# A two-layer attention trunk: accumulator tiles by token tile, grouped value products, earlier pairs, an ordered end

## The chip, the cores and the metric

The kernel runs on one core of one Trainium2 chip. The metric is the device time of one execution in microseconds (us); the median of several executions is compared. The profile shown is of one execution.

## What is computed

Two decoder layers over 256 tokens with 1024 features, in float32. Each layer normalises its input, multiplies it with one wide input projection, and cuts the result into heads of 64 columns:

```python
def even_layer(x, mem, norm_g, w_in, qk_g, sinks, mem_norm_g, w_mem_kv, w_out):
    h = rms_norm(x, norm_g)
    aq, ak, av, bq, bk, bv, mq, z = split_cols(h @ w_in, EVEN_SPLIT)
    ...
    y = jnp.concatenate([ya, yb, ym], axis=-1) * jax.nn.silu(z)
    return x + y @ w_out

def odd_layer(x, mem, norm_g, w_in, qk_g, b_f, mem_norm_g, w_mem_kv, w_out):
    h = rms_norm(x, norm_g)
    cq, ck, cv, cf, mq, z = split_cols(h @ w_in, ODD_SPLIT)
    ...
    y = jnp.concatenate([yc, ym], axis=-1) * jax.nn.silu(z)
    return x + y @ w_out
```

Layer 0 has 6 heads of sliding-window attention (`ya`, two key and value heads), 6 heads of causal attention over one block of 256 (`yb`) and 4 heads that look at a memory of 256 rows (`ym`). Layer 1 has 12 heads of forgetting attention (`yc`) and again 4 memory heads. Queries and keys are normalised per head; the head outputs are multiplied by the SiLU of the gate `z`, and an output projection adds into the residual.

## The kernel before

**Projections.** All projections are cut into chunks of up to 512 columns (`ch0` to `ch3`, `z0`, `z1`, `mem0`, `mem1`, `out00`, `out01` for layer 0; `cfmq`, `y1`, `va`, `qka`, `qb`, `kb`, `vb`, `y0`, `out10`, `out11` for layer 1). The 1024 rows of the contraction are eight blocks of 128 (k = 0 to 7), and a chunk is four pieces of two blocks. `emit_dma` loads a piece, `emit_prep` splits it into a rounded part and a rest (a ScalarE cast, L276, and a VectorE subtraction, L277), and `emit_mm` multiplies it. Tokens are two tiles of 128 (t = 0, 1). For each block and token tile there are three TensorE products of 512 columns: rounded by rounded (L315), rounded by rest (L316), rest by rounded (L317). A chunk accumulates in one PSUM tile `acc` of 128x2x512, two banks, from a pool with two buffers. In a chunk's first and last piece the products of t = 0 stand ahead of those of t = 1. After the last piece the chunk's `post` function reads `acc`.

**Pairs of heads.** Attention goes by pairs of heads, 16 of them: `a0` to `a2`, `b0` to `b2`, `m00`, `m01` in layer 0, `m10`, `m11`, `c0` to `c5` in layer 1. A pair has three units of work: `scores` (TensorE products, VectorE minimum, ScalarE exponential), `transp` (TensorE transposes of the probabilities of head f = 0 and f = 1, each copied by ScalarE into a tile `pT`, L531), and `values`. There, each head's products have 64 output rows, so that f = 0 goes to the lower and f = 1 to the upper half of the columns of the array; each of the four products (two key tiles kt, two heads) is two records in the trace. Then GpSimd scales the gate (L550), TensorE transposes it (L554), ScalarE copies the values out (L556), VectorE multiplies (L557), and the result is split into `yT` hi and lo (L193, L194), which the output projection reads, one block k for each pair.

**Order.** Units stand in a queue `units`; after each piece one or two are taken off (`pump`), and ahead of a piece of an output projection as many as it needs. A pair's `transp` and `values` are put into the queue when the next pair is added (`add_pair`) or when `end_pairs` is called, which happens after `mem0` and after `kb`. In layer 1 that means that `m11` waits in `pend` until `c4` is added (after `qka`), and `c5` until `c0` is added (after `kb`). The last projection takes its pieces alternately from `out10` and `out11`, in the order of blocks (6, 7), (4, 5), (0, 1), (2, 3); blocks 0 to 3 are pairs `c0` to `c3`.

A planner then fixes the order of every engine's instructions: it simulates the engines, and gives an engine the instruction that is ready and stands first in the source. Once fixed, the order on an engine does not change on the chip. [...]

Of the kernel before, what the change touches and what calls it, by code (L numbers as in the profile page):

```python
# [2 lines left out]

# [6 lines left out]
F32 = mybir.dt.float32  # L10
F32R = mybir.dt.float32r
AF = mybir.ActivationFunctionType
# [4 lines left out]
P = 128  # L17
# [32 lines left out]
def tile_hybrid_trunk(  # L50
# [13 lines left out]
    qkp = ctx.enter_context(tc.tile_pool(name="qkp", bufs=2))  # L64
    wk = ctx.enter_context(tc.tile_pool(name="wk", bufs=2))
    st = ctx.enter_context(tc.tile_pool(name="st", bufs=3))
    ps_acc = ctx.enter_context(tc.tile_pool(name="ps_acc", bufs=2, space=PSUM))
    ps_at = ctx.enter_context(tc.tile_pool(name="ps_at", bufs=4, space=PSUM))

    nc.scalar.preload_act_table_set("natural_log_exp_and_others")  # L70


    ident = const.tile([P, P], F32, name="ident")
# [220 lines left out]
    def emit_mm(i):  # L294
        c, p = pieces[i]
        hi, lo = preps.pop(i)
        aT = c.act()
        if p == 0:
            c.acc = ps_acc.tile([P, 2, 512], F32, tag="acc", name=f"acc_{c.name}")
        ks = range(c.kts[p][0], c.kts[p][1] + 1)  # L300
        steps = [(j, k, t) for j, k in enumerate(ks) for t in range(2)]
        if p in (0, NPIECE - 1):
            steps.sort(key=lambda x: x[2])
        for j, k, t in steps:
            a_hi = aT[0][:, k, t * P:(t + 1) * P]
            a_lo = aT[1][:, k, t * P:(t + 1) * P]
            o = c.acc[:, t, :c.n]
            first = p == 0 and j == 0
            last = p == NPIECE - 1 and j == PIECE_KT - 1

            parts = 2 if last and t == 1 and i == len(pieces) - 1 else 1
            w = c.n // parts
            for q in range(parts):
                qq = slice(q * w, (q + 1) * w)
                nc.tensor.matmul(o[:, qq], a_hi, hi[:, j, qq], start=first, stop=False)  # L315
                nc.tensor.matmul(o[:, qq], a_hi, lo[:, j, qq], start=False, stop=False)  # L316
                nc.tensor.matmul(o[:, qq], a_lo, hi[:, j, qq], start=False,  # L317
                                 stop=last and q == parts - 1)
        if p == NPIECE - 1:
            with tc.high_priority(offset=POST):  # L320
                c.post(c.acc)


    def qk_post(acc, c0, n, cs, rms, name, blocks, perm_a=False, mid=None):
        w = n * HD
        sq = wk.tile([P, 2, 512], F32, tag="sq", bufs=SQ_BUFS, name=f"qsq_{name}")
        nc.scalar.activation(sq[:, :, :w], acc[:, :, c0:c0 + w], AF.Square)
        if mid:
            mid()
        ss = st.tile([P, 2, n], F32, tag="ss", name=f"qss_{name}")  # L330
        nc.vector.tensor_reduce(ss, sq[:, :, :w].rearrange("p t (h d) -> p t h d", d=HD),
                                axis=AX.X, op=ALU.add)
        v = st.tile([P, 2 * n], F32, tag="vv", name=f"qv_{name}")
        for t in range(2):
            nc.vector.scalar_tensor_tensor(v[:, t * n:(t + 1) * n], ss[:, t, :],
                                           rms.ev[:, t:t + 1], cs[:, :n],
                                           op0=ALU.add, op1=ALU.mult)
        r = rsqrt_(v, 2 * n, name)
        qn = wk.tile([P, 2, 512], F32, tag="sq", bufs=SQ_BUFS, name=f"qn_{name}")
        r3 = r.rearrange("p (t h) -> p t h", t=2)  # L340
        for t in range(2):
            rb = r3[:, t, :, None].broadcast_to([P, n, HD])
            src = acc[:, t, c0:c0 + w].rearrange("p (h d) -> p h d", d=HD)
            if perm_a:
                dst = qn[:, t, 0:384].rearrange("p (i f d) -> p f i d", f=2, d=HD)
                for f in range(2):
                    nc.vector.tensor_mul(dst[:, f], src[:, 3 * f:3 * f + 3, :],
                                         rb[:, 3 * f:3 * f + 3, :])
                nc.vector.tensor_mul(qn[:, t, 384:512].rearrange("p (h d) -> p h d", d=HD),
                                     src[:, 6:8, :], rb[:, 6:8, :])  # L350
            else:
                nc.vector.tensor_mul(qn[:, t, :w].rearrange("p (h d) -> p h d", d=HD), src, rb)  # L352
        b0 = 0
        for kind, key, nb, gain in blocks:
            for g in range(0, nb, 2):
                m = min(2, nb - g)
                tp = ps_at.tile([P, 2, 256], F32, tag="at", name=f"qt_{name}_{b0}_{g}")
                for j in range(m):
                    for t in range(2):
                        b = b0 + g + j  # L360
                        nc.tensor.transpose(tp[:, j, t * P:(t + 1) * P],
                                            qn[:, t, b * P:(b + 1) * P], ident)
                (q_parts if kind == "q" else k_parts)(key, g, tp, m, gain)
            b0 += nb
# [57 lines left out]

    def v_post(acc, c0, n, rms, dst):
        for t in range(2):
            nc.vector.tensor_scalar_mul(dst[:, t, :], acc[:, t, c0:c0 + n], rms.r[:, t:t + 1])

    def silu_post(acc, rms, zs):
        for t in range(2):
            nc.vector.tensor_scalar_mul(zs[:, t, :], acc[:, t, :], rms.r[:, t:t + 1])
        s = wk.tile([P, 2, 512], F32, tag="sq", bufs=SQ_BUFS, name="sg")  # L430
        nc.scalar.activation(s, zs, AF.Exp, scale=-1.0)
        nc.scalar.activation(s, s, AF.Ln, bias=ones_c)
        nc.scalar.activation(s, s, AF.Exp, scale=-1.0)
        nc.vector.tensor_mul(zs, zs, s)  # L434
# [5 lines left out]
    def pump(n=1):  # L440
        while n > 0 and units:
            ready, fn = units[0]
            if not ready():
                return
            units.pop(0)
            fn()
            n -= 1
# [15 lines left out]
    class Pair:  # L463
# [70 lines left out]
        def values(self):  # L534
# [2 lines left out]
            nc.vector.reciprocal(rec, self.sums)  # L537
            o = ps_at.tile([P, 2, 256], F32, tag="at", name=f"o_{self.name}")
            v = self.v()
            for kt in range(2):  # L540
                q0 = 0 if (full or kt == 0) else P
                for f in range(2):
                    c = self.vcols[f]
                    nc.tensor.matmul(o[f * HD:(f + 1) * HD, 0, q0:256], v[:, kt, c:c + HD],  # L544
                                     self.pT[f][:, 256 * kt:256 * kt + 256 - q0],
                                     start=kt == 0, stop=kt == 1)
            zs = wk.tile([P, 2, P], F32, tag="zs", name=f"zs_{self.name}")
            zsil = zsils[self.layer]
            for t in range(2):
# [78 lines left out]
    def post_out(layer, half):  # L628
        def f(acc):
            dst = xt[:, :, 512 * half:512 * half + 512]  # L630
            if layer == 1:
                for t in range(2):
                    parts = 2 if half == 1 and t == 1 else 1
                    w = 512 // parts
                    for q in range(parts):
                        qq = slice(q * w, (q + 1) * w)
                        tag, b = ("pT", PT_BUFS) if half and t else ("p", 4)
                        o = wk.tile([P, 512], F32, tag=tag, name=f"o_{half}_{t}_{q}", bufs=b)
                        nc.vector.tensor_add(o[:, :w], acc[:, t, qq], dst[:, t, qq])
                        nc.sync.dma_start(out[t * P:(t + 1) * P,  # L640
                                              512 * half + q * w:512 * half + (q + 1) * w],
                                          o[:, :w])
                return
# [3 lines left out]
            with tc.high_priority(offset=HOIST):  # L647
                for j in range(2):
                    cc = slice(256 * j, 256 * j + 256)
                    nc.vector.tensor_add(dst[:, :, cc], acc[:, :, cc], dst[:, :, cc])  # L650
                    hi = turn_x1(hTs[1], 4 * half + 2 * j)
                with tc.issue_after(hi.ins):
                    for t in range(2):
# [11 lines left out]
    def post_cfmq(acc):  # L665
        xf = st.tile([P, 2, 12], F32, tag="f1", name="xf", bufs=1)
        for t in range(2):
            nc.vector.scalar_tensor_tensor(xf[:, t, :], acc[:, t, 0:12], R[1].r[:, t:t + 1], bfc,
                                           op0=ALU.mult, op1=ALU.add)
        qk_post(acc, 12, 4, cs_one, R[1], "cfmq", [("q", "mq1", 2, gq[:, 8:9])])  # L670
        add_mem_pairs(1, lambda: "y1" in done)
        a = st.tile([P, 2, 12], F32, tag="f2", name="fa", bufs=1)
        nc.vector.scalar_tensor_tensor(a, xf, -1.0, xf, op0=ALU.mult, op1=ALU.max)
        e = st.tile([P, 2, 12], F32, tag="f3", name="fe", bufs=1)
# [36 lines left out]
    def post_qka(acc):  # L711
        qk_post(acc, 0, 8, cs_one, R[1], "qka",
                [("q", "qa", 2, gq[:, 6:7]), ("k", "ka", 2, gcol[:, 7:8])])
        for j in (4, 5):
            add_fox(j, "qa", "ka", lambda: T["va"], j - 4)

    def post_va(acc):
        T["va"] = qkp.tile([P, 2, 256], F32, tag="mv", name="va", bufs=3)
# [94 lines left out]
    for i in range(len(pieces)):  # L813
# [21 lines left out]
        if c.name.startswith("out"):  # L835
            need = [f"o{c.name[3]}_{k}" for k in c.kts[p]]
            while not all(n in done for n in need):
                before = len(units)
                pump(1)
                assert len(units) < before  # L840
        emit_mm(i)
        pump(2 if len(units) > BACKLOG else 1)


# [28 lines left out]
```

## Time and profile before

| | |
|---|---|
| median of 3 runs | 294.77 us (294.49 to 295.39) |
| the profiled execution | 294.83 us |
| its span, first to last instruction | 293.1 us |
| TensorE busy | 283.6 us, 97% |
| VectorE busy | 217.4 us, 74% |
| ScalarE busy | 210.1 us, 72% |
| GpSimd busy | 49.1 us, 17% |
| mean granted TensorE clock | 0.998 of full speed |

The span is 1.7 us shorter than the execution's own time. Engine names are PE (TensorE products), PEld (its weight loads), DVE (VectorE), ACT (ScalarE), POOL (GpSimd), SP (the queue that issues the weight loads and the stores). A busy PE counts overlapping products once; the time from one product's start to the next one's start tells what a product really takes from the engine.

### The profile page before, as it was taken

How to read it: one execution, taken by the hardware profiler on the slowest of the kernel's cores; microseconds unless marked ns; L12 is line 12 of the kernel's file. 1: busy time of each engine (PE TensorE's matmuls, PEld its weight loads, DVE VectorE, ACT ScalarE, POOL GpSimd, SP SyncE). 2: the span in 40 equal slices, each digit the busy share in tenths (PEclk: the TensorE clock that was granted, in tenths of full speed). 3: DMA queues.
4: the chain of work that ended last, by engine and by line, in shares of the span. 5: the costliest groups of instructions: out<-in, count | busy, mean ns of one | idle time of the engine just before them, and what ended most of it. 6: DMA issues, size and time to landing. Idle time of an engine off the chain costs nothing.

```text
span 293.1 us, 4507 instructions
## 1 busy us (share of the span) xinstructions
PE 283.6 (97%) x1479; PEld 225.9 (77%) x1479; DVE 217.4 (74%) x474; ACT 210.1 (72%) x435; POOL 49.1 (17%) x113
## 2 busy tenths in 40 slices
PE   7799999999999999999999999999999999999993
PEld 4568887888787777877678989878887788777773
DVE  2567999879997986795638889958698789645423
ACT  3667895999779959767627649956678799668520
POOL 9920000000501000291000000460100220012100
PEclk9999999999999999999999999999999999999999
DMA  6967746442625362443126456586635524630003
GB/s 205 307 226 267 219 144 215 145 143 93 205 72 193 91 202 83 144 145 110 41 73 196 130 158 200 130 261 166 197 104 184 147 70 144 215 114 33 0 2 143
DMA packets 24871, 43.37 MB, mean 148 GB/s; under 512 B 1904, under 2 KB 6288, under 8 KB 24848
## 3 DMA queue, kind: packets, MB, share of 16 engines
q1 hardware_dynamic: 24544, 43.05, 47.0%
q0 software_dynamic: 288, 0.03, 0.5%
q8 instruction: 12, 0.20, 0.2%
q14 instruction: 11, 0.09, 0.1%
q10 hardware_dynamic: 16, 0.00, 0.0%
HBM read 42.02 MB, written 1.05 MB: 147 GB/s over the span
## 4 chain that ended last, share of the span: by engine, by line
PE 82%; DMA 7%; DVE 5%; ACT 2%; issue 2%; SPq 0%; DVEq 0%; ACTq 0%
DMA raw_ch<-in_e_w_in_dram 6%; PE acc_out L315 5%; PE acc_out L317 5%; PE acc_out L316 5%; PE acc_mem L315 3%; PE acc_ch L315 3%; PE acc_ch L317 3%; PE acc_y L316 3%; PE acc_ch L316 3%; PE acc_y L315 2%; PE acc_mem L317 2%; PE acc_mem L316 2%; PE acc_y L317 2%; PE o_c L544 2%; DVE wlo_ch L277 2%; PE o_m L544 2%
## 5 line engine op out<-in xcount | busy, mean ns | idle before, releaser
L277 DVE TENSOR_TENSOR wlo_ch<-raw_ch,whi_ch 128x1024 fp32r<-128x1024 f32 (+1 forms) x17 | 19.7, 1165 | 12.5 <-ACT whi_ch L276 12.4
L315 PE MATMUL acc_out<-whi_out,yT_hi 128*128 128x512 f32 (+1 forms) x65 | 26.3, 404 | 0.0
L316 PE MATMUL acc_ch<-wlo_ch,hT_hi 128*128 128x512 f32 x64 | 25.4, 397 | 0.6 <-DVE wlo_ch L277 0.6
L277 DVE TENSOR_TENSOR wlo_out<-raw_out,whi_out 128x1024 fp32r<-128x1024 f32 x16 | 20.4, 1280 | 7.2 <-ACT whi_out L276 7.1
L316 PE MATMUL acc_out<-wlo_out,yT_hi 128*128 128x512 f32 (+1 forms) x65 | 25.7, 396 | 0.0
L315 PE MATMUL acc_ch<-whi_ch,hT_hi 128*128 128x512 f32 x64 | 25.3, 396 | 0.2 <-DVE qn_ch L352 0.2
L317 PE MATMUL acc_ch<-whi_ch,hT_lo 128*128 128x512 f32 x64 | 25.4, 397 | 0.0
L317 PE MATMUL acc_out<-whi_out,yT_lo 128*128 128x512 f32 (+1 forms) x65 | 25.0, 397 | 0.0
L276 ACT CAST whi_ch<-raw_ch 128x1024 fp32r<-128x1024 f32 (+1 forms) x17 | 16.9, 994 | 9.9 <-DMA raw_ch<-in_e_w_in_dram 9.9
L276 ACT CAST whi_out<-raw_out 128x1024 fp32r<-128x1024 f32 x16 | 16.7, 1046 | 2.1 <-DMA raw_out<-in_o_w_out_dram 1.1
L509 ACT ACTIVATE p_c<-p_c,nm_c 128x128 f32<-128x128 f32 (+1 forms) x24 | 10.8, 451 | 5.8 <-DVE nm_c L502 5.8
L316 PEld LDWEIGHTS acc_ch<-wlo_ch,hT_hi 128*128 128x128 f32 x64 | 12.0, 188 | 3.6 <-DVE wlo_ch L277 1.3
L315 PEld LDWEIGHTS acc_out<-whi_out,yT_hi 128*128 128x128 f32 x65 | 12.2, 188 | 2.9 <-ACT yT_hi L193 0.4
L550 POOL TENSOR_TENSOR zs_c<-z,rec_c 128x128 f32<-128x128 f32 x12 | 5.5, 485 | 53.6 <-DVE z L434 26.3
L315 PEld LDWEIGHTS acc_ch<-whi_ch,hT_hi 128*128 128x128 f32 x64 | 12.0, 188 | 3.0 <-issue 0.6
L317 PEld LDWEIGHTS acc_out<-whi_out,yT_lo 128*128 128x128 f32 x65 | 12.2, 188 | 2.8 <-issue 0.4
L317 PEld LDWEIGHTS acc_ch<-whi_ch,hT_lo 128*128 128x128 f32 x64 | 12.0, 188 | 2.9 <-issue 0.4
L316 PEld LDWEIGHTS acc_out<-wlo_out,yT_hi 128*128 128x128 f32 x65 | 12.3, 189 | 2.5 <-issue 0.4
L550 POOL TENSOR_TENSOR zs_a<-z,rec_a 128x128 f32<-128x128 f32 x6 | 4.2, 727 | 56.7 <-PE acc_ch L317 56.4
L315 PE MATMUL acc_mem<-whi_mem,hmT_hi 128*128 128x512 f32 x32 | 12.9, 403 | 0.0
L315 PE MATMUL acc_z<-whi_z,hT_hi 128*128 128x512 f32 x32 | 12.9, 402 | 0.0
L316 PE MATMUL acc_z<-wlo_z,hT_hi 128*128 128x512 f32 x32 | 12.7, 398 | 0.0
(380 smaller groups left out, 880.7 us busy)
## 6 DMA issues: line engine op xcount, KB each, us to landing
raw_ch<-in_e_w_in_dram SPq DMA_DIRECT2D x15, 512.0 KB, 4.5
raw_z<-in_e_w_in_dram SPq DMA_DIRECT2D x8, 512.0 KB, 4.0
raw_y<-in_o_w_in_dram SPq DMA_DIRECT2D x8, 512.0 KB, 3.7
raw_out<-in_o_w_out_dram SPq DMA_DIRECT2D x8, 512.0 KB, 3.9
raw_mem<-in_e_w_mem_kv_dram SPq DMA_DIRECT2D x4, 512.0 KB, 3.4
raw_mem<-in_o_w_mem_kv_dram SPq DMA_DIRECT2D x4, 512.0 KB, 3.4
raw_out<-in_e_w_out_dram SPq DMA_DIRECT2D x4, 512.0 KB, 3.7
raw_qka<-in_o_w_in_dram SPq DMA_DIRECT2D x8, 256.0 KB, 3.0
```

The lines of the kernel that those rows point to most:

```text
L276: op = nc.scalar.copy(hi[:, jj, :c.n], raw[:, jj, :c.n])
L277: nc.vector.tensor_sub(lo[:, jj, :c.n], raw[:, jj, :c.n], hi[:, jj, :c.n].bitcast(F32))
L315: nc.tensor.matmul(o[:, qq], a_hi, hi[:, j, qq], start=first, stop=False)
L316: nc.tensor.matmul(o[:, qq], a_hi, lo[:, j, qq], start=False, stop=False)
L317: nc.tensor.matmul(o[:, qq], a_lo, hi[:, j, qq], start=False, stop=last and q == parts - 1)
L509: nc.scalar.activation(pt[:, a:b], src[:, a:b], AF.Exp, scale=-1.0, bias=nm[:, f, t:t + 1], accum_out=sums[:, f, t:t + 1])
L544: nc.tensor.matmul(o[f * HD:(f + 1) * HD, 0, q0:256], v[:, kt, c:c + HD], self.pT[f][:, 256 * kt:256 * kt + 256 - q0], start=kt == 0, stop ...
L550: nc.gpsimd.tensor_mul(zs[:, t, :].rearrange("p (f d) -> p f d", d=HD), self.zsel(zsil, t), rec[:, :, t:t + 1].broadcast_to([P, 2, HD]))
```

## The change

Four things. The accumulator `acc` becomes two tiles of 128x512, one for each token tile, from a pool of four one-bank buffers; whatever reads `acc` for both token tiles in one instruction becomes two instructions (the squares of `qk_post`, the residual addition of layer 0). In `values` the first product is that of kt = 0, f = 1, and the other three are told to the planner as standing behind it on TensorE. `end_pairs` is also called after the memory pairs of layer 1 and after `qka`. The last two pieces (blocks 2 and 3 of `out10` and `out11`) and their stores are emitted together under `in_order`, which ties each instruction to the one before it on its engine, in source order.

```diff
-    ps_acc = ctx.enter_context(tc.tile_pool(name="ps_acc", bufs=2, space=PSUM))
+    ps_acc = ctx.enter_context(tc.tile_pool(name="ps_acc", bufs=4, space=PSUM))
...
+    @contextmanager
+    def in_order():
+
+        traced = nc.cur_bb.bb.instructions
+        n = len(traced)
+        yield
+        last = {}
+        for i in traced[n:]:
+            if i.engine in last:
+                tc.add_manual_dep(
+                    i, last[i.engine],
+                    mybir.DependencyInfo(mybir.DependencyClass.NoSync,
+                                         mybir.DependencyReason.DATA),
+                    reason="in_order")
+            last[i.engine] = i.name
...
-            c.acc = ps_acc.tile([P, 2, 512], F32, tag="acc", name=f"acc_{c.name}")
+            c.acc = [ps_acc.tile([P, 512], F32, tag="acc", name=f"acc_{c.name}_{t}")
+                     for t in range(2)]
...
-            o = c.acc[:, t, :c.n]
+            o = c.acc[t][:, :c.n]
...
-        nc.scalar.activation(sq[:, :, :w], acc[:, :, c0:c0 + w], AF.Square)
+        for t in range(2):
+            nc.scalar.activation(sq[:, t, :w], acc[t][:, c0:c0 + w], AF.Square)
...
-            for kt in range(2):
+
+            def value(kt, f):
                 q0 = 0 if (full or kt == 0) else P
-                for f in range(2):
-                    c = self.vcols[f]
-                    nc.tensor.matmul(o[f * HD:(f + 1) * HD, 0, q0:256], v[:, kt, c:c + HD],
-                                     self.pT[f][:, 256 * kt:256 * kt + 256 - q0],
-                                     start=kt == 0, stop=kt == 1)
+                c = self.vcols[f]
+                return nc.tensor.matmul(o[f * HD:(f + 1) * HD, 0, q0:256], v[:, kt, c:c + HD],
+                                        self.pT[f][:, 256 * kt:256 * kt + 256 - q0],
+                                        start=kt == 0, stop=kt == 1)
+
+            lead = value(0, 1)
+            with tc.issue_after(lead.ins):
+                value(0, 0)
+                value(1, 1)
+                value(1, 0)
...
-                    nc.vector.tensor_add(dst[:, :, cc], acc[:, :, cc], dst[:, :, cc])
+                    for t in range(2):
+                        nc.vector.tensor_add(dst[:, t, cc], acc[t][:, cc], dst[:, t, cc])
...
         add_mem_pairs(1, lambda: "y1" in done)
+        end_pairs()
...
             add_fox(j, "qa", "ka", lambda: T["va"], j - 4)
+        end_pairs()
...
-        emit_mm(i)
-        pump(2 if len(units) > BACKLOG else 1)
+        if i < len(pieces) - 2:
+            emit_mm(i)
+            pump(2 if len(units) > BACKLOG else 1)
+
+    n = len(pieces)
+    with in_order():
+        emit_mm(n - 2)
+        emit_mm(n - 1)
```

The remaining lines of the diff only follow the new shape of `acc` (`acc[:, t, ...]` becomes `acc[t][:, ...]`).

## Rows read from the trace of the kernel before

**Rows 1.** The page's first part: busy time, share of span, instructions.

```profile
PE 283.6 (97%) x1479; PEld 225.9 (77%) x1479; DVE 217.4 (74%) x474; ACT 210.1 (72%) x435; POOL 49.1 (17%) x113
```

**Rows 2.** Busy time by stretch: stretch, length, engines with instructions, clock, DMA share, GB/s.

```profile
60.00:100.00 40.00, 40.00 (x210) 31.71 (x208) 35.78 (x89) 35.89 (x80) 5.47 (x10) 1.00 0.43 138
...
190.00:224.00 34.00, 34.00 (x178) 27.53 (x177) 25.92 (x44) 22.50 (x38) 7.39 (x10) 1.00 0.65 200
...
282.00:293.10 11.10, 6.60 (x36) 4.96 (x31) 3.49 (x7) 0.78 (x2) 0.00 (x0) 0.96 0.26 96
```

**Rows 3.** The waits of PE: total us, times, longest us.

```profile
PE tp_x L222 <- DMA xt<-in_x_dram: 2.1, 2, 1.4
```

**Rows 4.** Timeline of PE around one pair's values: start, length, instruction.

```profile
101.16 0.40 PE L315 MATMUL acc_z<-whi_z,hT_hi 128*128 128x512 f32 x1
101.49 0.65 PE L544 MATMUL o_b<-pT_b,bv 128*64 128x256 f32 x2
102.06 0.51 PE L316 MATMUL acc_z<-wlo_z,hT_hi 128*128 128x512 f32 x1
102.41 0.40 PE L317 MATMUL acc_z<-whi_z,hT_lo 128*128 128x512 f32 x1
102.64 0.40 PE L315 MATMUL acc_z<-whi_z,hT_hi 128*128 128x512 f32 x1
...
105.50 0.86 PE L544 MATMUL o_b<-pT_b,bv 128*64 128x256 f32 x6
```

**Rows 5.** Chain of waits, value products: end of the piece before, share of path, records.

```profile
66.28 0.80 PE o_a L544 x8
...
74.62 0.58 PE o_a L544 x2
...
76.54 0.79 PE o_a L544 x5
...
274.41 0.57 PE o_c L544 x2
```

**Rows 6.** Groups by line and shape, ACT and DVE: count, busy us, mean ns.

```profile
L327 ACT ACTIVATE qsq_qka<-acc_qka 128x1024 f32<-128x1024 f32 x1 | 1.0, 1027 | 1.7 <-PE acc_qka L317 1.7
...
L327 ACT ACTIVATE qsq_cfmq<-acc_cfmq 128x512 f32<-128x512 f32 x1 | 0.6, 592 | 0.0
...
L650 DVE TENSOR_TENSOR xt<-acc_out,xt 128x512 f32<-128x512 f32 x4 | 2.6, 686 | 1.7 <-PE acc_out L317 1.7
...
L639 DVE TENSOR_TENSOR o<-acc_out,xt 128x256 f32<-128x256 f32 x2 | 0.7, 414 | 0.0
```

**Rows 7.** Timeline near 47 us, PE at the start of chunk ch2.

```profile
46.51 1.02 DVE L352 TENSOR_TENSOR qn_ch<-acc_ch,r_ch 128x384 f32<-128x384 f32 x2
...
47.08 0.40 PE L317 MATMUL acc_z<-whi_z,hT_lo 128*128 128x512 f32 x1
...
47.68 0.47 PE L315 MATMUL acc_ch<-whi_ch,hT_hi 128*128 128x512 f32 x1 [0.21 <-DVE qn_ch L352]
```

**Rows 8.** Timeline of the last pair, from its values to its first use.

```profile
281.56 0.87 PE L544 MATMUL o_c<-pT_c,vb 128*64 128x256 f32 x8
...
282.56 0.48 PE L315 MATMUL acc_out<-whi_out,yT_hi 128*128 128x512 f32 x1
...
283.57 0.63 PE L317 MATMUL acc_out<-whi_out,yT_lo 128*128 128x512 f32 x2
283.76 0.41 ACT L193 CAST yT_hi<-ob_c 128x256 fp32r<-128x256 f32 x1 [0.49 <-DVE ob_c L557]
284.19 0.43 DVE L194 TENSOR_TENSOR yT_lo<-ob_c,yT_hi 128x256 fp32r<-128x256 f32 x1 [0.47 <-ACT yT_hi L193]
...
284.21 0.50 PE L315 MATMUL acc_out<-whi_out,yT_hi 128*128 128x512 f32 x1
```

**Rows 9.** Timeline of the end: last product, last additions, stores.

```profile
287.76 2.92 SPq L640 DMA_DIRECT2D out_dram<-o  x5
...
288.34 0.28 PE L317 MATMUL acc_out<-whi_out,yT_lo 128*128 128x256 f32 x1
288.65 1.35 DVE L639 TENSOR_TENSOR o<-acc_out,xt 128x512 f32<-128x512 f32 x3 [0.33 <-PE acc_out L317]
```

More of the change, by code (lines that the diff above doesn't have):

```diff
@@ L1 @@
 import math
-from contextlib import ExitStack
+from contextlib import ExitStack, contextmanager
 import concourse.bass as bass
@@ L342, in qk_post @@
             rb = r3[:, t, :, None].broadcast_to([P, n, HD])
-            src = acc[:, t, c0:c0 + w].rearrange("p (h d) -> p h d", d=HD)
+            src = acc[t][:, c0:c0 + w].rearrange("p (h d) -> p h d", d=HD)
             if perm_a:
@@ L424, in v_post @@
         for t in range(2):
-            nc.vector.tensor_scalar_mul(dst[:, t, :], acc[:, t, c0:c0 + n], rms.r[:, t:t + 1])
+            nc.vector.tensor_scalar_mul(dst[:, t, :], acc[t][:, c0:c0 + n], rms.r[:, t:t + 1])
     def silu_post(acc, rms, zs):
         for t in range(2):
-            nc.vector.tensor_scalar_mul(zs[:, t, :], acc[:, t, :], rms.r[:, t:t + 1])
+            nc.vector.tensor_scalar_mul(zs[:, t, :], acc[t], rms.r[:, t:t + 1])
         s = wk.tile([P, 2, 512], F32, tag="sq", bufs=SQ_BUFS, name="sg")
@@ L638, in f @@
                         o = wk.tile([P, 512], F32, tag=tag, name=f"o_{half}_{t}_{q}", bufs=b)
-                        nc.vector.tensor_add(o[:, :w], acc[:, t, qq], dst[:, t, qq])
+                        nc.vector.tensor_add(o[:, :w], acc[t][:, qq], dst[:, t, qq])
                         nc.sync.dma_start(out[t * P:(t + 1) * P,
@@ L667, in post_cfmq @@
         for t in range(2):
-            nc.vector.scalar_tensor_tensor(xf[:, t, :], acc[:, t, 0:12], R[1].r[:, t:t + 1], bfc,
+            nc.vector.scalar_tensor_tensor(xf[:, t, :], acc[t][:, 0:12], R[1].r[:, t:t + 1], bfc,
                                            op0=ALU.mult, op1=ALU.add)
```

## The prediction

> **What bounds the kernel now.** I read the busy times first, then the waits of PE, then the chain of waits, then the timeline where PE works least well. TensorE is busy 283.6 of 293.1 us [rows 1], and its largest wait is 2.1 us, for the input at the start [rows 3]. From 60 to 100 us it is busy for all of 40.00 us [rows 2]. So the time is TensorE's work, a start of about 10 us and a tail of some 4.5 us after the last product [rows 9]. Work taken off TensorE counts in full as long as no other engine takes its place; work taken off another engine counts only at the start, at the tail, or where PE waits for it.
>
> A busy PE is not one that works well. In the chain of waits a pair's four value products come in two forms. All eight records together take 0.80 us (`a0`, at 66.28). In the other form two records, which are one product, stand alone at 74.62 and take 0.58 us, and the other three products follow at 76.54 and take 0.79 us [rows 5]. Three products take as long as four: the two heads' products lie in different halves of the array's columns and run side by side, so a lone one leaves half the array empty and finds no partner later. 11 of the 16 pairs are split like this in the chain of waits, from 74.62 to 274.41 [rows 5]: `a1` and `a2`, all three b, both memory pairs of layer 0, and four c. The reason is in the source: the first product needs only head 0's `pT`, so the planner starts it before head 1's copy is there, and then fills with projection products, which stand earlier.
>
> **The change part by part.**
>
> *Value products together.* The new first product needs head 1's `pT`, the later of the two copies; the other three are then ready and stand next in source order, so nothing should come between. A lone product in the middle of projection products costs more than its 0.57 us (101.49 to 102.06): the step into it is 0.33 us (101.16 to 101.49) where two projection products lie 0.23 us apart (102.41 to 102.64), and the first step after it is 0.35 us (102.06 to 102.41) [rows 4]. From 101.16 to 102.41 are 1.25 us; less two projection products of 0.23, it is 0.79 us. Three of the 11 lone products have projection products on both sides (0.79 each); at eight the work on one side is other attention work, and I count only the lone product and one step, 0.57 + 0.10 = 0.67. Sum: 3 x 0.79 + 8 x 0.67 = 7.7 us less. The bounds: nothing, if the planner splits them again, and 11 x 0.79 = 8.7 us, if every lone product cost as much as the one in rows 4. I take 7.7.
>
> [...]
>
> *What the new wait costs.* The first product now waits for ScalarE's second copy. Behind it on PE stand the other three and then all projection products, so if ScalarE is later on the chip than in the plan, PE stands still. The trace has this wait already, since the later three products of every split pair need the same copy, and the waits of PE show none for it; the one row of these waits that is above 2 us is the input's [rows 3]. I take nothing; the far bound is a rival below.
>
> *Accumulator by token tile.* Ten squares are cut in two. One of 128x1024 takes 1.03 us, one of 128x512 0.59 [rows 6], so each cut costs 2 x 0.59 - 1.03 = 0.15 us, some 1.5 us of ScalarE in all. ScalarE is idle for 83 us of the span [rows 1], so over most of it this is hidden behind projection products. It is not so sure from 60 to 100 us, where ScalarE is busy 35.89 and VectorE 35.78 of 40 us [rows 2]: two of the joined pairs lie there, and if PE needs 1.3 us less, the two have 38.7 us for work that grew by the squares of that stretch. There I let half of the gain be lost, 0.7 us (bounds: nothing, and all 1.3). The four residual additions of layer 0 become eight, 0.41 instead of 0.69 us each [rows 6]; those of t = 0 can run while the products of t = 1 do, and for the last, 0.41 replaces 0.69, but one more stands ahead. Between 0.28 us less and 0.14 us more (8 x 0.41 against 4 x 0.69 is 0.52 more, of which I count the last pair of additions, a quarter); I take nothing. A gain, too: near 47 us the first product of `ch2` waits until both multiplications that read `ch1`'s tile are over (46.51 to 47.53), 0.60 us after the product before, where 0.23 is usual [rows 7]. With a tile for each t it needs only the first. I take 0.3 us less (bounds 0 and 0.37).
>
> *Pairs that do not wait.* Two units of `m11` and two of `c5` come some pieces earlier: transposes, copies, products, the gate's scaling and the split. No DMA is among them, and none of these instructions is new. They leave the crowded last third for 190 to 224 us, where ScalarE is busy 22.50 of 34 us [rows 2]. PE has no idle time there to fill, so its sum stays: nothing. If that cover were missing, two pairs' copies would cost about 1 us.
>
> *The last products in source order.* Now each of the last two pieces runs t = 0 with blocks 2 and 3, then t = 1. Block 3 is the last pair. At present, from 282.56 to block 3's first product at 284.21, PE fills with six products of block 2, the last two from 283.57; with 0.23 us for each they are through at 284.03, so PE stands still for some 0.2 us [rows 8]. In source order only three such products stand ahead of block 3's: PE would be through at about 282.56 + 0.3 + 2 x 0.23 = 283.3 and wait until 284.21, 0.9 us. So the order costs 0.9 - 0.2 = 0.7 us (bounds: nothing, if products of earlier blocks are still left, and 1.65, if none fill). What it gives back: now three additions, of 512, 256 and 256 columns, run after the last product, 288.65 to 290.00 [rows 9]. In the new order the first of them belongs to t = 0 of `out11`, whose products end some 1.4 us (six products) before the end, and the second to the first half of the last product; only the last addition, 0.41 us [rows 6], is left. 1.35 - 0.41 = 0.94 us less (bounds: 0, if the stores, 2.92 us of issue for five, hold up the end, and 0.94). SP holds nothing else then, and the five stores keep their order.
>
> *Sum.* -7.7 - 0.3 - 0.9 + 0.7 + 0.7 = -7.5 us. The profiled execution took 294.83 us, 0.06 above the median of the runs, so the new time is 287.3 us.
>
> **The rivals.**
>
> *Half comes through.* Half of the joins' gain goes, because the planner still puts other work between the four products of some pairs, or because ScalarE and VectorE take over as the bound also beyond 60 to 100 us. For it speaks that these two are near 90% there [rows 2], against it that the five whole pairs of before are not torn apart once ready. 287.3 + 3.85 = 291.1 us.
>
> *The lead stands alone again.* The planner places the first product and then earlier-standing projection products, and the other three later. Then 11 lone products stay and perhaps the five whole pairs split as well. With as many as before, what is left is -0.3 - 0.9 + 0.7 = -0.5: 294.3 us, within 0.3%. That is the rival in which the change does not do what it says.
>
> [...]
>
> *Slower: the lead's wait.* PE stands before the lead until ScalarE's second copy is done, because the plan thinks the copy earlier than it is. At 16 pairs it decides from 7.5 / 16 = 0.47 us a pair; at 0.6 us a pair the time is 294.8 - 7.5 + 9.6 = 296.9 us. For it speaks that a fixed order cannot step aside; against it that PE today shows no wait for these copies.
>
> **How the numbers follow.** Differences within 0.3%, 0.9 us, can hardly be told from no change here. Forecast 0.66; half comes through 0.16; the lead alone 0.07; the page's rule 0.02; slower 0.09. Faster is the first, second and fourth, 0.84; same 0.07; slower 0.09. The best bounds all at once, -8.7 - 0.4 - 0.9 - 0.3 = -10.3, give 284.5; I put the low end at 285.0. The high end is the case in which half comes through, 291.1, with some room: 291.4. What lies outside is the lone lead, the slower case and a little of the ends, about 2 in 10.
>
> **What the changed profile would show.** In the chain of waits and the timeline every pair has its four value products in one group of eight records, of 0.80 us for causal pairs; no group of two is left. PE's busy time falls by about 7 us and its waits stay small. Near the end, a wait of PE for `yT_hi` of about 0.9 us, and after the last product one addition of 256 columns alone. `ch2` starts without the gap near 47 us. Wrong would be: groups of two or six records, PE waits for `pT`, or a PE that is idle in 60 to 100 us.

## The result and the profile after

The new kernel takes 297.38 us (median of 9 runs, 295.67 to 298.74) against 295.28 us of the old one beside it (9 runs, 294.49 to 295.96). The ratio is 1.0069, 95% interval [1.0041, 1.0097]: slower by some 2 us. The forecast was 287.3 us, with 0.09 on "slower".

| us | before | after |
|---|---|---|
| the profiled execution | 294.83 | 298.68 |
| its span | 293.1 | 295.9 |
| PE busy | 283.6 | 279.1 |
| sum of PE's gaps over 0.06 us | 3.2 | 11.3 |
| start of the last product to the end | 4.79 | 4.03 |
| mean granted TensorE clock | 0.998 | 0.994 |

Three of these rows make up the whole difference of the spans: -4.5 busy, +8.1 in gaps and -0.76 in the tail are +2.8. So the profile answers half of the question at once: TensorE did get less to do, and it spent more than that standing still. Of the gaps 2.6 us before and 1.9 after lie in the first 25 us, where PE waits for its input. Of the busy time after, some 1.7 us are the price of a stretch at half clock (273 to 276.5 us, below), estimated from the clock of 0.51 granted there.

The page's first part and its clock line (one digit for each fortieth of the span), beside [rows 1]:

```profile
PE 279.1 (94%) x1479; PEld 225.6 (76%) x1479; DVE 216.4 (73%) x478; ACT 210.5 (71%) x445; POOL 49.1 (17%) x113
...
PEclk9999999999999999999999999999999999999899
```

The chain of waits after, value products only (end of the piece before, length, records), beside [rows 5]:

```profile
126.52 0.80 PE o_b L562 x8
...
207.29 1.01 PE o_m L562 x8
...
272.10 0.87 PE o_c L562 x8
...
282.03 0.80 PE o_c L562 x8
...
284.48 0.87 PE o_c L562 x8
```

All value products in this chain come in groups of eight records; counted over the whole trace, all 16 pairs do, where 11 were split before. The joins do what they say. Four products with the causal shape take 0.80 us (0.87 where PE had waited for them), and the price of a lone one is gone.

The waits of PE (total us, times, longest us). Before, the largest beside the two that stand ahead of the first projection product [rows 3] were these, and all others are 0.3 us or less:

```profile
PE acc_ch L316 <- DVE wlo_ch L277: 0.6, 1, 0.6
...
PE acc_ch L315 <- DVE qn_ch L352: 0.2, 1, 0.2
```

After:

```profile
PE o_c L562 <- ACT pT_c L549: 2.7, 2, 2.0
PE acc_out L332 <- ACT yT_hi L209: 2.4, 3, 1.3
...
PE tp_m L229 <- issue: 1.6, 1, 1.6
...
PE acc_cfmq L334 <- DVE hT_lo L220: 0.9, 1, 0.9
PE qt_ch L379 <- DVE qn_ch L370: 0.7, 1, 0.7
PE qt_ch L379 <- DVE qn_ch L365: 0.6, 1, 0.6
...
PE acc_mem L332 <- DVE z L447: 0.2, 1, 0.2
```

There is no single wait that replaces the work removed. Six rows make 8.9 us, at some nine places from 34 to 287 us, and their releasers are both ScalarE and VectorE. By stretch, beside [rows 2] (length, busy time of PE, PEld, DVE, ACT, POOL with instructions, clock, DMA share, GB/s):

```profile
60.00:100.00 40.00, 39.17 (x202) 31.77 (x201) 34.81 (x77) 34.77 (x74) 4.29 (x6) 1.00 0.44 145
257.00:282.00 25.00, 22.96 (x122) 18.46 (x120) 13.48 (x36) 16.35 (x42) 4.79 (x8) 0.93 0.19 65
282.00:295.90 13.90, 8.90 (x54) 6.53 (x53) 4.53 (x9) 2.21 (x6) 0.00 (x0) 1.00 0.20 75
273.00:276.50 3.50, 3.50 (x16) 3.31 (x17) 2.32 (x11) 1.82 (x6) 0.00 (x0) 0.51 0.00 0
```

From 257 to 282 us PE misses 2.04 us, all in one wait, while ScalarE is busy for 16.35 of 25 us: no engine is full there. The wait in the timeline after (start, length, instruction, idle time before it):

```profile
270.37 0.36 ACT L582 COPY ob_c<-o_c 128x256 f32<-128x256 f32 x1
...
270.62 1.05 ACT L292 CAST whi_out<-raw_out 128x1024 fp32r<-128x1024 f32 x1
...
271.57 0.48 ACT L549 COPY pT_c<-tp_c 128x384 f32<-128x384 f32 x1
...
272.10 0.87 PE L562 MATMUL o_c<-pT_c,vb 128*64 128x256 f32 x8 [2.04 <-ACT pT_c L549]
...
273.71 0.41 PE L505 MATMUL s_c<-u_kb,u_qb 128*128 128x256 f32 x1
273.93 0.42 PE L507 MATMUL s_c<-kl_kb,fox_qb 128*128 128x256 f32 x1
```

PE stands at the lead of a c pair. The transposes that its copy `pT` reads are through at 270.06 us, but the copy (271.57) lies in ScalarE's fixed order behind a weight cast of 1.05 us. PE's order is fixed too, and it starts nothing else from 270.06 to 272.10 us. This is the wait that the rival "the lead's wait" named, at two of the 16 pairs instead of all. After it, two products of 256 columns lie 0.22 us apart, at the clock of 0.51 in the 273 to 276.5 row above; at 46.3 us, at a clock of 1.00, it is 0.12 us.

### The profile page after: what moved, and what is told of

It reads as the page before. It is cut to its first block, busy times and chain, and to the rows that moved or that the text cites. A ratio compares the mean times of both kernels' runs of the same rounds, so it can differ in the third digit from the quotient of the medians.

```text
span 295.9 us, 4516 instructions
## 1 busy us (share of the span) xinstructions
PE 279.1 (94%) x1479; PEld 225.6 (76%) x1479; DVE 216.4 (73%) x478; ACT 210.5 (71%) x445; POOL 49.1 (17%) x113
## 3 DMA queue, kind: packets, MB, share of 16 engines
q1 hardware_dynamic: 24544, 43.05, 46.3%
HBM read 42.02 MB, written 1.05 MB: 146 GB/s over the span
## 4 chain that ended last, share of the span: by engine, by line
PE 54%; DVE 16%; ACT 14%; DMA 8%; issue 6%; SPq 0%; DVEq 0%; ACTq 0%
DMA raw_ch<-in_e_w_in_dram 6%; PE acc_out L332 4%; PE acc_out L333 4%; PE acc_out L334 3%; PE acc_y L332 2%; PE acc_y L334 2%; PE acc_y L333 2%; ACT whi_ch L292 2%; PE acc_mem L332 2%; ACT p_c L527 2%; PE acc_mem L334 2%; PE acc_mem L333 2%; DVE wlo_out L293 2%; DVE wlo_z L293 1%; DMA raw_z<-in_e_w_in_dram 1%
## 5 line engine op out<-in xcount | busy, mean ns | idle before, releaser
L292 ACT CAST whi_ch<-raw_ch 128x1024 fp32r<-128x1024 f32 (+1 forms) x17 | 16.7, 996 | 14.2 <-DMA raw_ch<-in_e_w_in_dram 13.8
L293 DVE TENSOR_TENSOR wlo_out<-raw_out,whi_out 128x1024 fp32r<-128x1024 f32 x16 | 19.7, 1239 | 9.0 <-ACT whi_out L292 8.9
L332 PE MATMUL acc_ch<-whi_ch,hT_hi 128*128 128x512 f32 x64 | 23.6, 397 | 0.0
L334 PE MATMUL acc_out<-whi_out,yT_lo 128*128 128x512 f32 (+1 forms) x65 | 23.2, 395 | 0.0
L576 POOL TENSOR_TENSOR zs_c<-z,rec_c 128x128 f32<-128x128 f32 x12 | 6.3, 549 | 42.7 <-DVE rec_c L555 21.0
L293 DVE TENSOR_TENSOR wlo_y<-raw_y,whi_y 128x1024 fp32r<-128x1024 f32 x8 | 9.6, 1224 | 4.7 <-ACT whi_y L292 4.6
L292 ACT CAST whi_y<-raw_y 128x1024 fp32r<-128x1024 f32 x8 | 8.3, 1065 | 6.4 <-DMA raw_y<-in_o_w_in_dram 3.3
```

What stands on the lines that cost most here:

```text
L292: op = nc.scalar.copy(hi[:, jj, :c.n], raw[:, jj, :c.n])
L293: nc.vector.tensor_sub(lo[:, jj, :c.n], raw[:, jj, :c.n], hi[:, jj, :c.n].bitcast(F32))
L576: nc.gpsimd.tensor_mul(zs[:, t, :].rearrange("p (f d) -> p f d", d=HD), self.zsel(zsil, t), rec[:, :, t:t + 1].broadcast_to([P, 2, HD]))
```

## The experiments

Each of the four parts was run alone, and each was taken out of the whole. Then the accumulators and the earlier pairs were cut further, and projection work was moved to a place where PE waits. Times are medians; "before" is the old kernel in the same series. Busy and gaps are of the profiled execution, its start included, and lone products are counted over its trace. The start differs from profile to profile: the gaps of its first 25 us lie between 0.95 and 4.1 us.

| kernel | us | before | ratio [95%] | PE busy | gaps | lone |
|---|---|---|---|---|---|---|
| joins alone | 291.51 | 295.13 | 0.988 [0.9814, 0.9947] | 276.9 | 6.4 | 0 |
| accumulators alone | 298.66 | 295.13 | 1.0105 [1.0056, 1.0155] | 285.3 | 4.0 | 11 |
| earlier pairs alone | 299.80 | 295.13 | 1.0139 [1.0093, 1.0185] | 287.7 | 4.2 | 14 |
| ordered end alone | 295.87 | 295.13 | 1.0012 [0.9982, 1.0042] | 284.4 | 2.8 | 11 |
| whole without joins | 301.91 | 294.80 | 1.0236 [1.02, 1.0271] | 287.2 | 7.2 | 16 |
| whole without accumulators | 293.87 | 294.80 | 0.9959 [0.9933, 0.9985] | 276.2 | 10.2 | 0 |
| whole without earlier pairs | 295.43 | 294.80 | 1.0027 [0.9996, 1.0058] | 278.1 | 11.2 | 0 |
| whole without ordered end | 296.73 | 294.80 | 1.0067 [1.004, 1.0095] | 276.8 | 11.4 | 0 |
| cut reads, old accumulator | 297.30 | 295.58 | 1.0069 [1.0031, 1.0107] | 285.1 | 4.4 | 13 |
| joins + first early call | 293.11 | 295.58 | 0.9911 [0.9879, 0.9943] | 278.0 | 6.4 | 0 |
| joins + second early call | 293.87 | 295.58 | 0.9945 [0.9921, 0.997] | 278.8 | 7.4 | 0 |
| joins + moved fill | 291.33 | 295.58 | 0.9862 [0.9833, 0.9891] | 276.0 | 6.8 | 0 |

The old kernel, the joins alone and the earlier pairs alone can be compared without the start: PE's order is the same up to the 97th product of the projections (at about 34 us), and 1349 products of all kinds run from it to the end. From there on PE is busy for 253.7 us and idle for 0.6 before, 246.5 and 4.9 with the joins alone, 256.7 and 2.4 with the earlier pairs alone.

### Joins alone

Only `values` is changed, in the old kernel:

```diff
-            for kt in range(2):
+            def value(kt, f):
...
+            lead = value(0, 1)
+            with tc.issue_after(lead.ins):
+                value(0, 0)
+                value(1, 1)
+                value(1, 0)
```

> Kernel before with only the value products grouped. Theory 1 (the joins are worth what was predicted, and what the whole change loses comes from the other parts): 287 to 289.5 us, all 16 pairs in groups of eight records, PE waits other than at the start under 1.5 us in all. Theory 2 (the grouped products make PE wait for head 1's copy, and this wait eats the gain): 293 us or more, with PE waits for pT of some 0.4 us a pair.

Measured: 0.988 of before, 3.6 us faster by the medians, the best of the four parts and faster than both kernels. The time lies between the two theories, and the waits are above the 1.5 us that the first allowed. PE busy fell by 6.7 us (7.1 from the 97th product on), near the 7.7 of the prediction. The gaps rose from 3.2 to 6.4 us, and, leaving out those at the start, from 1.2 to 5.5. The waits of PE in this kernel:

```profile
PE acc_out L315 <- ACT yT_hi L193: 1.6, 1, 1.6
PE acc_mem L315 <- DVE z L429: 1.3, 1, 1.3
...
PE o_c L543 <- ACT pT_c L531: 0.6, 1, 0.6
PE tp_c L528 <- ACT pT_c L531: 0.6, 1, 0.6
```

The largest in its timeline:

```profile
147.43 0.71 PE L317 MATMUL acc_out<-whi_out,yT_lo 128*128 128x512 f32 x2
...
148.80 0.42 DVE L564 TENSOR_TENSOR ob_m<-ob_m,o_m 128x256 f32<-128x256 f32 x1
149.25 0.40 ACT L193 CAST yT_hi<-ob_m 128x256 fp32r<-128x256 f32 x1 [1.17 <-DVE ob_m L564]
...
149.71 0.50 PE L315 MATMUL acc_out<-whi_out,yT_hi 128*128 128x512 f32 x1 [1.57 <-ACT yT_hi L193]
```

PE has used up its products when the last pair of layer 0 is still on its way through ScalarE and VectorE; ScalarE itself waits 1.17 us there. Counting the products of the projections in the two traces (963 in each) shows where the gain goes. At the 449th PE is 5.3 us ahead of the old kernel (143.4 against 148.7), at the first of layer 1 it is 2.1 ahead (155.2 against 157.3). At the 897th it is 6.2 ahead (259.3 against 265.5), at the last one 3.4 (284.9 against 288.3). Not all of that is given back: in the new order attention products that stood ahead of these marks stand behind them. Of the 3.2 us between the first two marks 1.6 are PE's idle time and 1.7 such work; of the 2.8 us between the last two, 1.3 and 1.5. So the waits at the ends of the two layers, where a chain over three engines leads and not TensorE's work, take 2.9 us. With the wait of `mem1`'s first product for `z1`'s buffer (1.28 us at 108.7) they are nearly all of the 4.3 us by which PE's idle time grew.

### Accumulators alone

```diff
-            c.acc = ps_acc.tile([P, 2, 512], F32, tag="acc", name=f"acc_{c.name}")
+            c.acc = [ps_acc.tile([P, 512], F32, tag="acc", name=f"acc_{c.name}_{t}")
+                     for t in range(2)]
...
-        nc.scalar.activation(sq[:, :, :w], acc[:, :, c0:c0 + w], AF.Square)
+        for t in range(2):
+            nc.scalar.activation(sq[:, t, :w], acc[t][:, c0:c0 + w], AF.Square)
```

> Kernel before with only the accumulator as a tile for each token tile. Theory 1: slower, 296 to 298 us, because the planner's new order puts the first attention products and the memory's transposes ahead of projection products near 47 us, with a PE wait of about 1.5 us there, and more such waits later. Theory 2: within 1 us of before, 294 to 295.5 us, since the loss lies in the grouped products.

Measured: 1.0105, some 3.1 us slower, where the prediction had 0.3 us faster; a little above the first theory, whose wait near 47 us is there. The waits of PE:

```profile
PE tp_m L229 <- issue: 1.1, 1, 1.1
PE acc_cfmq L334 <- DVE hT_lo L220: 0.9, 1, 0.9
...
PE qt_ch L379 <- DVE qn_ch L365: 0.6, 1, 0.6
PE qt_ch L379 <- DVE qn_ch L370: 0.4, 1, 0.4
```

These four rows are 3.0 us. They stand in the waits of the whole change too, with 3.8 us, and none of them, above 0.1 us, in those of before. The first lies where the prediction saw a gain, near 47 us [rows 7]. The timeline of the whole change there:

```profile
47.17 1.22 DVE L293 TENSOR_TENSOR wlo_ch<-raw_ch,whi_ch 128x1024 fp32r<-128x1024 f32 x1
...
48.98 0.48 DVE L520 CUSTOM_DVE_ANT_0 p_a<-s_a,mask_a,negsink 128x256 f32<-128x256 f32 x1
...
49.39 1.02 DVE L370 TENSOR_TENSOR qn_ch<-acc_ch,r_ch 128x384 f32<-128x384 f32 x2
49.57 0.63 PE L229 MATMUL tp_m<-ident,memt 128*128 128x128 f32 x4 [1.57 <-issue]
...
50.09 0.47 PE L332 MATMUL acc_ch<-whi_ch,hT_hi 128*128 128x512 f32 x1
```

The gap of 0.21 us at `ch2`'s first product (50.09) is gone: it follows the first of the two multiplications, not the second. But the order is another one. On VectorE `ch1`'s multiplication stands behind a weight split and two minimums and starts at 49.39 instead of 46.51. On PE the transposes of the memory (`tp_m`) stand ahead of `ch2`, and start 0.11 us after the second minimum ends (49.46). The distance is the same with accumulators alone (48.21 and 48.32). That fits a wait for the buffer of the scores that this minimum reads (in the source both tiles come from `ps_at`), which I did not test by itself. The end is longer as well: in the planner's new order all five last additions run together, from 290.23 to 292.77 us, and from the start of the last product to the end it takes 5.17 us (4.79 before).

### Earlier pairs alone

```diff
         add_mem_pairs(1, lambda: "y1" in done)
+        end_pairs()
...
             add_fox(j, "qa", "ka", lambda: T["va"], j - 4)
+        end_pairs()
```

> Kernel before with only the two added calls of end_pairs in layer 1. Theory 1: work moves and none goes, 294 to 296 us; with the last pairs nearer to the end of the projections the last stage may lose up to 1 us. Theory 2: the same.

Measured: 1.0139, some 4 us slower, where the prediction and both theories had nothing or 1 us at most. The trace has 14 lone products instead of 11: `m11`, `c0` and `c3`, whole before, are among the split ones. At 0.67 us these three are 2.0 of the 4.1 us by which PE busy grew. Another 1.3 us lie in the first 78 products, which this part doesn't touch: in this execution the granted clock was 0.50 from 9.6 to 13.0 us. The waits show two new stops:

```profile
PE acc_vb L315 <- DVE qn_qb L352: 1.2, 1, 1.2
PE acc_out L315 <- ACT yT_hi L193: 0.5, 1, 0.5
```

Where the rest is lost can't be read from marks. This kernel is 5.3 us behind the old one at the 817th projection product, 0.5 at the 897th and 5.2 at the last, but attention products have changed places with the marks: behind the 897th stand 74 of them here and 55 in the old kernel.

### Ordered end alone

```diff
+    n = len(pieces)
+    with in_order():
+        emit_mm(n - 2)
+        emit_mm(n - 1)
```

> Kernel before with only the last two pieces in source order. By the predicted terms: 0.7 us lost before the last pair's first use and 0.9 gained in the additions, 294.5 us. Theory 1 with a costlier end: 295.5 to 297 us, with a PE wait for yT_hi of 1 us or more near 284 us. Theory 2: as predicted, 294.5 us.

Measured: 1.0012 with an interval over 1, no difference. The timeline of its end:

```profile
283.95 0.50 PE L332 MATMUL acc_out<-whi_out,yT_hi 128*128 128x512 f32 x1 [0.71 <-ACT yT_hi L210]
...
288.79 0.28 PE L334 MATMUL acc_out<-whi_out,yT_lo 128*128 128x256 f32 x1
289.10 1.35 DVE L656 TENSOR_TENSOR o<-acc_out,xt 128x512 f32<-128x512 f32 x3 [1.47 <-PE acc_out L334]
```

The wait for `yT_hi` came as forecast (0.71 us; the prediction had 0.9). The gain at the additions did not: with one accumulator for both token tiles, the additions of `out11` all wait for its last product, and three follow it as before [rows 9]. The two parts need each other: from the start of the last product to the end it takes 4.80 us here, 5.17 with the accumulators alone and 4.03 with both.

### One part taken out of the whole

Four kernels undo one part of the change each, by the reverse of the diffs above; of the one without the earlier pairs that is all:

```diff
         add_mem_pairs(1, lambda: "y1" in done)
-        end_pairs()
...
-        end_pairs()
```

> The changed kernel with the value products as before. Theory 1 (joins gain, the rest loses): slower than the changed kernel by about 5 us or more, 302 us. Theory 2 (the grouped products cost back what they save): as the changed kernel or faster, 297 us or less.

> The changed kernel with the accumulator of both token tiles as before. Theory 1: the wait near 47 us and its followers go, 289 to 292 us. Theory 2: within 1 us of the changed kernel, 296.5 to 298 us.

> The changed kernel without the two added calls of end_pairs. Theory 1: within 1.5 us of the changed kernel, 296 to 298.5 us. Theory 2: the same.

> The changed kernel with the last two pieces left to the planner. Theory 1: the wait for yT_hi near 286 us goes and an addition or two come back after the last product, so within 1 us of the changed kernel, 296.5 to 298 us. If the ordered end is the main loss: 293 us or less.

Measured, by the ratios in the table times 295 us, against the 1.0069 of the whole: without the joins the kernel is 4.9 us slower still; without the accumulators it is 3.2 us faster, and then beats the old kernel (0.9959); without the earlier pairs 1.2 us faster, with intervals that overlap; without the ordered end no different. Without the joins there are 16 lone products in 13 pairs (in `m11` all four stand alone), more than the old kernel's 11, so the joins hide part of what the other parts do. The kernel without the accumulators has the 0.2 us gap at `ch2`'s first product again and none of the four waits of the accumulator part; its time is still 1.9 us above the range that its first theory gave. The others came as expected, the one without the earlier pairs 0.6 us below its range.

### Cut reads on the old accumulator

The squares and the residual additions are cut in two, and the tile stays one of two banks:

```diff
-        nc.scalar.activation(sq[:, :, :w], acc[:, :, c0:c0 + w], AF.Square)
+        for t in range(2):
+            nc.scalar.activation(sq[:, t, :w], acc[:, t, c0:c0 + w], AF.Square)
...
-                    nc.vector.tensor_add(dst[:, :, cc], acc[:, :, cc], dst[:, :, cc])
+                    for t in range(2):
+                        nc.vector.tensor_add(dst[:, t, cc], acc[:, t, cc], dst[:, t, cc])
```

> Kernel before, accumulator left as one tile, but the squares and the residual additions cut in two as in the change. If the extra instructions are what the accumulator's part costs: 297.5 to 299 us, as with the whole part. If the separate tiles and the planner's new order with them cost it: 294.5 to 296 us, with none of the PE waits near 48 us and 160 us.

Measured: 1.0069, 2.0 us of the accumulator part's 3.1 by the ratios. The time lies between the two forecasts, near the first. Two of the four waits are there without any new tile:

```profile
PE tp_m L213 <- PE acc_z L317: 0.7, 1, 0.7
PE acc_cfmq L317 <- DVE hT_lo L204: 0.6, 1, 0.6
```

The two further waits, for `qn_ch`, come only with the tiles (above 0.12 us). The intervals of the two kernels overlap, so the share of the cut reads is known roughly. It isn't the price of the instructions by themselves, since the order changed with them: 13 products stand alone instead of 11. The longer squares do not fill ScalarE: it is busy 211.2 us here against 210.1 before, 71% of the span.

### One early call at a time, beside the joins

Joins alone plus the first call, and joins alone plus the second:

```diff
         add_mem_pairs(1, lambda: "y1" in done)
+        end_pairs()
```

```diff
             add_fox(j, "qa", "ka", lambda: T["va"], j - 4)
+        end_pairs()
```

> Grouped value products and only the first added call of end_pairs (m11 earlier). If the pairs' part costs by work that crowds ScalarE and VectorE from 200 to 226 us: about 291.5 to 292 us, since the qb chunk's chain is hardly touched by m11 alone. If it costs by lone products alone, the same as with grouped products alone, 291.5 us.

> Grouped value products and only the second added call (c5 earlier). If the order of the last stage is what costs: 293 us or more, with PE waits for pT of c pairs after 260 us of 1.5 us or more. If the pairs' part costs by lone products alone: 291.5 us.

Measured: 0.9911 and 0.9945 where joins alone had 0.988. The interval of joins alone reaches over both, and the profiles show that little of it is the calls' doing. Up to the 211th projection product the three kernels have the same order on PE. At the 193rd the one with the first call is already 0.9 us behind joins alone (62.1 against 61.2 us; its granted clock was 0.50 from 10.4 to 13.8 us), and at the end it is 1.0 us behind: that the first call costs anything is not shown, though its 293.11 us lie above both forecasts. The one with the second call is 1.9 us behind at that product and 2.8 at the end, which leaves 0.9 us for the call.

With the second call PE waits for `pT_c` 1.07 us at 270.2 and 0.63 us at 281.1, as its first forecast had it, where joins alone have 0.57 us (at a transpose, 266.5) and 0.62 us. The first is the place of the 2.04 us in the whole change; without either call the whole still has 1.16 us there (272.6), so the call lengthens this wait and is not all of it.

### Joins with the fill moved

If PE only lacks work at the end of layer 0, projection pieces kept back for that place should take the 1.57 us. The pieces of `mem1` go between the third and the fourth of `out00` (and what builds the tiles of the next chunks follows them):

```diff
+    moved = [q for q in pieces if q[0].name == "mem1"]
+    pieces[:] = [q for q in pieces if q[0].name != "mem1"]
+    at = [i for i, q in enumerate(pieces) if q[0].name == "out00"][3]
+    pieces[at:at] = moved
...
-        if c.name == "out00" and p == 0:
+        if c.name == "out00" and p == 3:
```

> Grouped value products, and the chunk mem1 moved to stand between the third and the fourth piece of out00, so that projection products are left while the last memory pair of layer 0 is finished. If grouped products lose their gain where PE runs out of projection products: the PE wait of 1.57 us for yT_hi near 150 us goes and the time falls by 1 to 2 us to 289.5 to 290.5 us. If the gain is lost elsewhere: 291 to 292 us, or slower by the new order.

Measured: 0.9862 against 0.988 of joins alone, no difference that can be told, and 291.33 us where the second forecast had 291 to 292. The waits of PE:

```profile
PE acc_out L315 <- DVE z L429: 1.3, 1, 1.3
...
PE o_m L543 <- ACT pT_m L531: 0.7, 1, 0.7
PE tp_m L528 <- ACT pT_m L531: 0.7, 1, 0.7
PE o_c L543 <- ACT pT_c L531: 0.6, 1, 0.6
```

The wait for `yT_hi` near 150 us is gone, and two new ones, 1.42 us together, stand at 132.9 and 134.3 us, from where the fill was taken. Fill moved is a wait moved; it does not say that more fill would not help.

## Why the prediction was wrong

**What bounds the kernel.** "Work taken off TensorE counts in full as long as no other engine takes its place" was the step that failed. No other engine took its place: ScalarE and VectorE have 71% and 73% of the span. What took it are chains over three engines. In the old kernel those chains just fitted behind PE's work, in an order that was fixed beforehand: after its 97th projection product PE was idle for 0.6 us, with the joins alone for 4.9. Each change to the list of instructions gives the planner another list, and another order on all engines, in places far from the edit. Of the 1479 places in PE's order 474 hold another product than before (by name and shape) with the joins alone, 945 with the accumulators alone, 327 with the earlier pairs, 12 with the ordered end. The loss goes not by this count but by whether a wait opens or a group of value products falls apart; that the new orders are worse is shown by the waits, why the planner prefers them is not.

**Value products together, -7.7.** Right in the mechanism: no lone product is left, and PE busy falls by 6.7 us with the joins alone. Four of the causal shape take 0.80 us on the path, and the records of the two heads start in pairs 7 ns apart (272.102 and 272.109 us). As a term of the time it was mis-sized: alone the joins gave 3.6 us, since PE's idle time grew by 4.3 beside it, and in the whole 4.9.

**The new wait, 0.** Wrong. PE waits 2.7 us for `pT_c` in the whole change, in two of 16 pairs, where the rival had 0.6 us at each. The old trace could not show it: at a split pair the lone product came early and the projections filled the time until the second copy. The row that I read as "no wait" [rows 3] showed the cover, and the joins remove the cover.

**60 to 100 us, +0.7.** PE misses 0.83 us there in the whole change (39.17 of 40.00), but 0.72 of it is the accumulators' wait for `qn_ch`. With the joins alone it is 0.09 us. The size was near, the cause another.

**Accumulators, -0.3.** The step that failed most: +3.2 us in the whole and +3.1 alone. Counted were the instructions (1.5 us hidden), and the gap near 47 us; both happened as said. Not counted was that the new order puts a stop of 1.57 us where the old had one of 0.21, and three more behind it: four waits of 3.0 us alone and 3.8 in the whole, about the size of the loss.

**Earlier pairs, 0.** Wrong: +4.1 alone, +1.2 in the whole. "PE has no idle time there to fill, so its sum stays" held neither for the sum (three whole pairs fell apart, and PE is busy 3.0 us longer from the 97th projection product on) nor for the waits (1.2 and 0.5 us).

**The ordered end.** Right in both halves. PE waits for `yT_hi` 0.65 us (0.9 forecast), and the tail is 0.76 us shorter (0.94 forecast). The timeline after, beside [rows 8, 9]:

```profile
286.62 0.40 ACT L209 CAST yT_hi<-ob_c 128x256 fp32r<-128x256 f32 x1 [0.49 <-DVE ob_c L583]
...
287.07 0.50 PE L332 MATMUL acc_out<-whi_out,yT_hi 128*128 128x512 f32 x1 [0.65 <-ACT yT_hi L209]
...
290.82 0.69 DVE L665 TENSOR_TENSOR o<-acc_out,xt 128x512 f32<-128x512 f32 x1 [0.67 <-PE acc_out L334]
...
291.89 0.28 PE L334 MATMUL acc_out<-whi_out,yT_lo 128*128 128x256 f32 x1
292.21 0.76 DVE L665 TENSOR_TENSOR o<-acc_out,xt 128x256 f32<-128x256 f32 x2 [0.69 <-PE acc_out L334]
```

The addition of 512 columns runs before the last product, as forecast. What is left behind it is 0.76 us in two instructions, not 0.41 in one. Gain and cost cancel, as the kernel without this part shows.

**The rivals.** The time came near that of the slower rival (296.9), and two of the three signs that the prediction gave as "wrong" are there: PE waits for `pT`, and a PE that is idle from 60 to 100 us. The rival's mechanism has 2.7 us of it, though, a third of the 8.1, so that its time was met is luck. "Half comes through" describes the joins taken alone, 291.5 us, but not by its reasons: no projection products between the four, no engine at its bound. For the fourth chance in the list, 0.02, no run shows a reason: with the joins no lone product is left, and the four products of a causal pair take 0.80 us.

**The sum.** By the ratios, the parts alone are -3.5, +3.1, +4.1 and +0.4, together +4.1, and the whole is +2.0: they overlap by 2 us, part of which are the lone products that the other parts add and the joins remove.

**What stays open.** Why the planner's new orders open these waits; about 1.0 us of PE busy time with the earlier pairs alone that no lone product explains, and as much with the accumulators alone (there 0.7 of the 1.7 us lie in the first 78 products, up to 23 us); how much of the accumulators' cost lies in the cut reads and how much in the tiles; and what the earlier pairs cost in the whole, where 1.2 us is within the intervals. Taking its waits out one at a time was not tried.

## What to carry to other kernels

In a kernel whose order is fixed by a plan, a busy share of 97% is a property of that order, not of the work: before an edit is priced at nothing, look at which chain over several engines ends just behind the bound engine's last filler, since here the gain was lost there. Run each part of a combined change alone, and out of the whole: here one part alone gave 3.6 us and two others cost 3.1 and 4.1, and the kernel to keep is the joins alone (291.51 us). A wait absent from a profile says nothing about a wait whose cover the change removes.

## What the runs showed that was not expected

TensorE's granted clock fell to half within the work. In the profile after it is 0.51 of full from 273 to 276.5 us and 1.00 on both sides, and the fall comes about 1 us after PE's idle time of 2.04 us. By an estimate from that clock, some 3.4 us at half of it are 1.7 us lost. If the wait brought the fall about, it cost twice in this execution, once as idle time and once more as slow products; one profile does not show that it did.

Of the nine runs of the new kernel five have a mean clock of 0.994 and 297.38 to 298.74 us, four have 1.000 and 295.67 to 296.38: about 2 us between their means, 298.1 and 296.1. The second group is still above the old kernel's 295.28. That all five lost their clock at this wait is not shown, since only one of them was profiled and a mean does not tell the place. Other kernels have low means too, the old one down to 0.988 (297.68 us, in the series of the joins alone), and in the profiles of the earlier pairs alone and of the joins with either early call the clock was at half near the start, from about 10 to 13 us.

A wait of 2.05 us at 272.35 in the profile of the kernel without the ordered end was followed by no fall (clock 1.00 from 270 to 276), so the length of the wait alone does not decide here.
